# All splits of the streamed weights on VectorE, instead of one in eight (one in six) on GpSimd

## The chip, the cores and the metric

The kernel runs on one core of a Trainium2 chip. The metric is the device time in microseconds (us) of one execution. The engines that matter are TensorE (PE in the views; its weight loads are PEld), VectorE (DVE), ScalarE (ACT), GpSimd (POOL) and SyncE (SP), whose queue issues nearly all transfers. SBUF is the on-chip memory, PSUM the accumulators that TensorE writes.

## The reference

One sequence of 256 rows of width 1024, in float32, goes through two blocks. The first has two layers: retention, then differential attention, each with attention to a memory of 256 rows beside it and a feed-forward part behind it. The second has a mixer of a gated delta rule and a gated linear attention, a cross-attention, and an MLP. Cut to what matters:

```python
for layer in range(2):
    u = rms_norm(x, attn_norm_w[layer]) @ w_in[layer]
    o_main = retention(...) or diff_attention(...)          # chunks of 64 rows
    o_mem = memory_attention(qc, mk, mv)
    x = x + concatenate([o_main, o_mem]) @ w_out[layer]
    gu = rms_norm(x, ffn_norm_w[layer]) @ w_gate_up[layer]
    x = x + (silu(gu[..., :2816]) * gu[..., 2816:]) @ w_down[layer]
# second block
proj = rmsnorm(x, norm_mix_g) @ w_in
qkv = silu(causal_depthwise_conv(concatenate([gq, gk_, gv]), gdn_conv_w))   # four taps
o_a = gated_delta_rule_chunked(q_a, k_a, v_a, g_a, beta_a)
o_b = gla_chunked(q_b, k_b, v_b, log_fg)
merged = sigmoid(gate_a) * y_a + sigmoid(gate_b) * y_b
x = x + merged @ w_out
x = x + cross_attention(x, mem) @ xattn_wo
x = x + square(relu(rmsnorm(x) @ mlp_w1)) @ mlp_w2
return rmsnorm(x, norm_final_g)
```

All products are wanted at float32 accuracy.

## The kernel before

**Weights.** Some 213 MB of weights come from HBM, each used once, in units of 128 x 2 x 512 numbers (two rows of blocks of 128, 512 columns). The function `unit` (L261) makes one: SyncE issues the transfer into a buffer `raw` (three of them), ScalarE casts it to the matmul's shorter float format as `hi` (L277; four buffers), and then `lo = raw - hi`, the remainder in the same format (four buffers), is made through the helper `tt` (L184, its instruction is L185). This last step is called the split here. TensorE then makes three products of each block with an activation that is split in the same way: hi with xh, lo with xh, hi with xl (`mm`, L207). `proj` (L290), `proj_T` and `proj_T2` loop over the units of one weight matrix, so TensorE goes through 12 or more matmuls for each unit.

**Who splits.** A counter `lo_count` chooses the engine of each split: GpSimd for every eighth unit (`share`), for every sixth from the mixer's convolution on (L782) until the mixer's end (L825); VectorE for the others. GpSimd's other work is the inverse roots (`rsqrt`, L200: a power on a few numbers for each row, named `tiny`), some masks (L1005) and fills, and two products of 128x1024.

**Order.** Each engine has a queue of its own and runs it in order. The program is written stage by stage, and a scheduler puts the instructions of each engine into an order before the kernel is built, from the data dependencies, the buffers and its own estimate of durations. So a change of one instruction's engine moves others.

**Held evacuations.** Three places (L432, L461, L677) call `later(instruction, n)`: the product that scales attention heads by their inverse root (T_699 is one, in `mem_kv`) is kept back on VectorE until the split of the n-th next unit, four for the first half of the rows and five for the second. They are released in `unit`, but in the kernel before only if that unit's split is itself on VectorE; if it is GpSimd's turn, they wait for the next unit.

**Names.** T, L, Z, B, G, H, V are work tiles in SBUF, `acc` and `ps` accumulators in PSUM, `constants` a tile with the identity and other fixed numbers. A `ps<-constants,...` matmul is a transpose (L210).

Of the kernel before, what the change touches and what calls it, by code (L numbers as in the profile page):

```python
# [34 lines left out]
class _Pack:  # L35
    def __init__(self):
        self.parts, self.at = [], 0
# [83 lines left out]
class _Builder:  # L121
    def __init__(self, ctx, tc, aps, names, stages):
        self.tc = tc
        self.nc = tc.nc
        self.a = dict(zip(names, aps))
        self.stages = stages
        self.n = self.np = 0
        ent = lambda name, bufs, **k: ctx.enter_context(tc.tile_pool(name=name, bufs=bufs, **k))
        self.cp = ent("const", 1)
        self.sp = ent("stream", 4)  # L130
        self.wp = ent("work", 1)
        self.tp = ent("tiny", 1)
        self.dp = ent("scratch", 2, space=bass.MemoryType.DRAM)
        self.pa = ent("acc", 4, space=PSUM)
        self.ps = ent("small", 2, space=PSUM)
        self.lo_count = 0
        self.mT2 = self.xv = self.xT = None
        self.share = 8
        self.n2 = 0
        self.units, self.held = 0, {}  # L140
        self.use('T', ('sm', 'pg'))
# [119 lines left out]
    def unit(self, w, k0, nk, cols):  # L261
        nc = self.nc
        W = sum(b for _, b in cols)
        self.n += 1
        n = self.n
        raw = self.sp.tile([P, 2, 512], F32, tag="raw", name=f"raw{n}", bufs=3)
        parts = [slice(0, 1), slice(1, 2)] if self.units == 0 else [slice(0, nk)]
        for k in parts:
            o = 0
            for c0, wd in cols:  # L270
                nc.sync.dma_start(out=raw[:, k, o:o + wd], in_=w[(k0 + k.start) * P:(k0 + k.stop) * P, c0:c0 + wd]
                                  .rearrange("(k p) c -> p k c", p=P))
                o += wd
        hi = self.sp.tile([P, 2, 512], F32R, tag="hi", name=f"hi{n}", bufs=4)
        lo = self.sp.tile([P, 2, 512], F32R, tag="lo", name=f"lo{n}", bufs=4)
        for k in parts:
            nc.scalar.copy(hi[:, k, :W], raw[:, k, :W])  # L277
        self.lo_count += 1
        eng = nc.gpsimd if self.lo_count % self.share == 0 else nc.vector
        for k in parts:  # L280
            last = self.tt(lo[:, k, :W], raw[:, k, :W], hi[:, k, :W].bitcast(F32), ALU.subtract, eng=eng)
        self.units += 1
        if eng is nc.vector:
            for u in [u for u in self.held if u <= self.units]:
                for i in self.held.pop(u):
                    self.tc.add_manual_dep(i, last.ins.name, mybir.DependencyInfo(
                        mybir.DependencyClass.NoSync, mybir.DependencyReason.DATA), reason="queued behind a split")
        return hi, lo

    def proj(self, hT, w, cols, order=None, meanwhile=None):  # L290
# [476 lines left out]
    def mixer(self):  # L767
        nc, w = self.nc, self.a['w_in_2'][0]
        ms, r = self.stats(self.x)
        xn = [self.big() for _ in range(2)]  # L770
        for t in range(2):
            for c in range(2):
                cc = slice(c * 512, (c + 1) * 512)
                self.ts(xn[t][:, cc], self.x[t][:, cc], r[:, t:t + 1])
        hT = self.x_T2('mix', 0, xn)
        hT[7]
        if self.mT2 is not None:
            self.xv = self.xattn_v(self.mT2)
        self.gates(hT)
        decays = [self.decays(g) for g in range(2)]  # L780
        self.use('G', ('sm',))
        self.share = 6  # L782
        z = [[self.conv(hT, w, kind, g) for kind in range(3)] for g in range(2)]
        on = []
        self.use('T', ('pg',))
        for g in range(2):
            on.append(self.gdn(g, z[g], *decays[g]))
        self.use('G', ('sm',))
        obn = self.gla(hT, w)
        oaT = []  # L790
        for g in range(2):
            a = self.proj(hT, w, [(3072 + g * 512, 512)])
            e = [self.t('L') for _ in range(2)]
            for t in range(2):
                self.act(e[t], a[t], AF.Tanh, scale=0.5)
                self.stt(e[t], e[t], 1.0, a[t], ALU.add, ALU.mult)
                self.tt(e[t], e[t], on[g][t])
            oaT += self.to_T(lambda t, f: e[t][:, f * P:(f + 1) * P], 4, 'Z', lambda f: self.col('gdn'))
        for c in range(2):
            a = self.proj(hT, w, [(6160 + c * 512, 512)])  # L800
            for t in range(2):
                e = self.t()
                self.act(e, a[t], AF.Tanh, scale=0.5)
                self.stt(e, e, 1.0, a[t], ALU.add, ALU.mult)
                self.tt(obn[t][c], obn[t][c], e)
        m = [[self.t('L') for _ in range(2)] for _ in range(2)]
        ga = [[self.t('L') for _ in range(2)] for _ in range(2)]
        for c0, d in ((8224, m), (7200, ga)):
            for c in range(2):
                g = self.proj(hT, w, [(c0 + c * 512, 512)])  # L810
                for t in range(2):
                    self.act(d[t][c], g[t], AF.Tanh, scale=0.5)
        for c in range(2):
            y = self.proj(oaT, self.a['w_branch_gdn_2'][0], [(c * 512, 512)])
            for t in range(2):
                self.stt(ga[t][c], ga[t][c], 1.0, y[t], ALU.add, ALU.mult)
        obT = self.to_T(lambda t, f: obn[t][f // 4][:, (f % 4) * P:(f % 4 + 1) * P], 8, 'H',
                        lambda f: self.col('gla', f % 2))
        for c in range(2):
            y = self.proj(obT, self.a['w_branch_gla_2'][0], [(c * 512, 512)])  # L820
            for t in range(2):
                self.stt(m[t][c], m[t][c], 1.0, y[t], ALU.add, ALU.mult)
                self.tt(m[t][c], m[t][c], ga[t][c], ALU.add)
        self.use('T', ('sm', 'pg'))
        self.share = 8  # L825
        mT = self.to_T(lambda t, f: m[t][f // 4][:, (f % 4) * P:(f % 4 + 1) * P], 8, 'Z')
        self.xT = self.out_proj(mT, self.a['w_out_2'][0], 0.5, gname='xat')

# [593 lines left out]
```

## Time and profile before

| | before |
|---|---|
| median of three timed runs | 1295.37 us (1294.4 to 1302.5) |
| the profiled execution's own time | 1287.81 us |
| its span | 1286.1 us |
| TensorE busy | 1250.5 us (97%) |
| TensorE weight loads | 1071.6 us (83%) |
| VectorE busy | 828.1 us (64%), 1299 instructions |
| ScalarE busy | 678.8 us (53%) |
| GpSimd busy | 180.9 us (14%), 115 instructions |

The profile is of one execution. A busy share is an average over stages with different limits: what a change is worth shows in the stretches in which TensorE stands still, and in what it waits for there.

### The profile page before, as it was taken

Reading aid. Unit: us, or ns where it says so; the run is one execution under the profiler, and the core shown is the slowest. Engines: PE = TensorE matmul, PEld = TensorE weight load, DVE = VectorE, ACT = ScalarE, POOL = GpSimd, SP = SyncE. Lnnn points to the kernel's source line nnn. Section 1 sums busy time; section 2 is a strip of 40 time slices with the busy share of each in tenths; the row PEclk is TensorE's granted clock in tenths of the full one; section 3 lists DMA queues with packets and bytes.
Section 4 is the critical chain, followed back from the end, with each engine's and each line's share of the span. In section 5 each row is a group of like instructions: output and inputs, shape, how many; then the busy total and the mean of one; then the engine's idle time right before and its main releaser. Section 6 shows DMA issues by size and latency. Waiting matters only on the chain.

```text
span 1286.1 us, 19034 instructions
## 1 busy us (share of the span) xinstructions
PE 1250.5 (97%) x7160; PEld 1071.6 (83%) x7160; DVE 828.1 (64%) x1299; ACT 678.8 (53%) x1088; POOL 180.9 (14%) x115
## 2 busy tenths in 40 slices
PE   8999999999999999999998999999999999999997
PEld 8787888888778888888878998867788897888886
DVE  6576677755876667674467787486635665788542
ACT  5655656545664565554467573343344444565442
POOL 0122110010420110100101021221111000001011
PEclk9999999999999999999999999999999999999999
DMA  8826566656644256665653545224365552565653
GB/s 297 279 87 203 176 196 185 196 195 192 187 131 148 83 164 201 192 190 189 195 176 115 181 121 170 84 70 142 112 194 175 172 177 86 166 207 178 201 190 107
DMA packets 147005, 215.72 MB, mean 168 GB/s; under 512 B 15456, under 2 KB 71904, under 8 KB 146912
## 3 DMA queue, kind: packets, MB, share of 16 engines
q1 hardware_dynamic: 146336, 213.27, 53.3%
q8 instruction: 56, 0.92, 0.3%
q10 hardware_dynamic: 432, 0.70, 0.2%
q0 software_dynamic: 144, 0.52, 0.1%
q14 instruction: 37, 0.30, 0.1%
HBM read 213.02 MB, written 1.44 MB: 167 GB/s over the span
## 4 chain that ended last, share of the span: by engine, by line
PE 84%; DVE 6%; DMA 3%; ACT 3%; issue 2%; POOL 1%; SPq 1%; POOLq 0%; ACTq 0%; DVEq 0%
PE acc L207 74%; PE ps L207 7%; PE ps L210 2%; DVE lo L185 2%; ACT hi L277 1%; DVE T L185 1%; DMA raw<-in_w_in_dram 1%; POOL tiny L200 1%; DVE L L185 1%; ACT T L195 1%; SPq L1053 0%; DMA constants<-in_small_dram 0%; DVE B L185 0%; DMA B<-in_mem_dram 0%; SPq L1029 0%
## 5 line engine op out<-in xcount | busy, mean ns | idle before, releaser
L277 ACT CAST hi<-raw 128x1024 fp32r<-128x1024 f32 (+1 forms) x393 | 407.1, 1039 | 413.3 <-PE acc L207 326.7
L185 DVE TENSOR_TENSOR lo<-raw,hi 128x1024 fp32r<-128x1024 f32 (+1 forms) x341 | 412.5, 1214 | 316.5 <-ACT hi L277 312.3
L207 PE MATMUL acc<-H,hi 128*128 128x512 f32 (+1 forms) x1696 | 470.5, 347 | 1.8 <-ACT hi L277 1.7
L207 PE MATMUL acc<-H,lo 128*128 128x256 f32 x1328 | 372.2, 281 | 0.0
L207 PEld LDWEIGHTS acc<-H,hi 128*128 128x128 f32 x1696 | 296.3, 190 | 43.7 <-ACT hi L277 2.5
L207 PEld LDWEIGHTS acc<-H,lo 128*128 128x128 f32 x1328 | 252.4, 190 | 1.8 <-issue 0.8
L185 POOL TENSOR_TENSOR lo<-raw,hi 128x1024 fp32r<-128x1024 f32 (+1 forms) x52 | 124.2, 2389 | 796.2 <-ACT hi L277 618.8
L207 PE MATMUL acc<-hi,H 128*128 128x512 f32 (+1 forms) x672 | 212.4, 392 | 1.2 <-ACT H L195 0.6
L207 PE MATMUL acc<-hi,Z 128*128 128x512 f32 x544 | 171.4, 391 | 0.0
L207 PE MATMUL acc<-hi,L 128*128 128x512 f32 x512 | 160.2, 390 | 0.0
L207 PEld LDWEIGHTS acc<-hi,H 128*128 128x128 f32 x672 | 125.3, 189 | 27.9 <-issue 1.8
L207 PE MATMUL acc<-lo,H 128*128 128x512 f32 (+1 forms) x336 | 131.6, 392 | 0.8 <-DVE lo L185 0.8
L207 PEld LDWEIGHTS acc<-hi,Z 128*128 128x128 f32 x544 | 102.1, 188 | 20.9
L207 PEld LDWEIGHTS acc<-hi,L 128*128 128x128 f32 x512 | 96.1, 188 | 19.8
L207 PE MATMUL acc<-lo,Z 128*128 128x512 f32 x272 | 106.0, 390 | 0.0
L207 PE MATMUL acc<-lo,L 128*128 128x512 f32 x256 | 99.7, 390 | 0.0
L207 PEld LDWEIGHTS acc<-lo,H 128*128 128x128 f32 x336 | 63.6, 189 | 14.6 <-DVE lo L185 1.7
L200 POOL TENSOR_TENSOR tiny<-tiny,constants 128x2 f32<-128x2 f32 (+4 forms) x41 | 41.4, 1012 | 238.6 <-DVE tiny L189 190.2
L207 PEld LDWEIGHTS acc<-lo,Z 128*128 128x128 f32 x272 | 51.1, 188 | 10.2
L207 PEld LDWEIGHTS acc<-lo,L 128*128 128x128 f32 x256 | 48.1, 188 | 9.8
L357 ACT COPY T<-acc 128x256 f32<-128x256 f32 x120 | 43.8, 369 | 12.8 <-PE acc L207 9.3
L185 DVE TENSOR_TENSOR T<-acc,T 128x256 f32<-128x256 f32 x120 | 44.9, 416 | 2.1 <-ACT T L357 2.1
(218 smaller groups left out, 1109.3 us busy)
## 6 DMA issues: line engine op xcount, KB each, us to landing
raw<-in_w_in_dram SPq DMA_DIRECT2D x91, 512.0 KB, 3.7
raw<-in_w_gate_up_dram SPq DMA_DIRECT2D x176, 256.0 KB, 3.4
raw<-in_mlp_w_dram SPq DMA_DIRECT2D x64, 512.0 KB, 4.3
raw<-in_w_down_dram SPq DMA_DIRECT2D x44, 512.0 KB, 4.5
raw<-in_w_out_dram SPq DMA_DIRECT2D x24, 512.0 KB, 4.3
raw<-in_w_in_dram SPq DMA_DIRECT2D x42, 256.0 KB, 3.9
raw<-in_w_mem_kv_dram SPq DMA_DIRECT2D x8, 512.0 KB, 3.9
raw<-in_xattn_wk_dram SPq DMA_DIRECT2D x8, 512.0 KB, 3.8
```

The lines of the kernel that those rows point to most:

```text
L185: return (eng or self.nc.vector).tensor_tensor(out=out, in0=a, in1=b, op=op)
L195: self.nc.scalar.activation(out, in_, f, scale=scale, bias=bias, **k)
L200: self.nc.gpsimd.tensor_tensor(out=out, in0=in_, in1=self.c('mhalf')[:, :n], op=ALU.pow)
L207: self.nc.tensor.matmul(out, lhsT, rhs, start=start, stop=stop, skip_group_check=True)
L210: self.nc.tensor.transpose(out, in_, self.ident[:in_.shape[0], :in_.shape[0]])
L277: nc.scalar.copy(hi[:, k, :W], raw[:, k, :W])
L357: self.nc.scalar.copy(out[:, a, :], accs[a][:, 1, :])
```

## The change

Every split is VectorE's. The counter and the two shares go, and with them the condition on the release of held evacuations, which now always come with the unit they were meant for. What is computed is the same.

```diff
@@ __init__
-        self.lo_count = 0
         self.mT2 = self.xv = self.xT = None
-        self.share = 8
@@ unit
         for k in parts:
             nc.scalar.copy(hi[:, k, :W], raw[:, k, :W])
-        self.lo_count += 1
-        eng = nc.gpsimd if self.lo_count % self.share == 0 else nc.vector
+        eng = nc.vector
         for k in parts:
             last = self.tt(lo[:, k, :W], raw[:, k, :W], hi[:, k, :W].bitcast(F32), ALU.subtract, eng=eng)
         self.units += 1
-        if eng is nc.vector:
-            for u in [u for u in self.held if u <= self.units]:
-                for i in self.held.pop(u):
-                    self.tc.add_manual_dep(...)
+        for u in [u for u in self.held if u <= self.units]:
+            for i in self.held.pop(u):
+                self.tc.add_manual_dep(...)
@@ mixer
-        self.share = 6
@@
-        self.share = 8
```

Fifty-two instructions move from GpSimd's queue to VectorE's, 51 of 128x1024 and one of 128x2x256. The numbers of instructions on TensorE, ScalarE and SyncE stay. Lines in the changed kernel are two lower up to L275 and four to six lower behind it. The scheduler's order changes in more places than the 52. Three of them follow.

First, VectorE's queue in the differential attention, at the softmax's scale factors (tiny_3387 scales T_3369, which TensorE then transposes into ps_3391). Before:

```order
L185 TENSOR_TENSOR Z_3347<-acc_3254,tiny_3345 128x512
L708 RECIPROCAL tiny_3387<-tiny_3372 128x2
L192 SCALAR_TENSOR_TENSOR tiny_3233<-tiny_3371 128x2
L451 TENSOR_REDUCE tiny_3410<-T_3404 128x2
L192 SCALAR_TENSOR_TENSOR tiny_3387<-tiny_3387,tiny_3230,tiny_3371 128x2
L189 TENSOR_SCALAR tiny_3410<-tiny_3410 128x2
L192 SCALAR_TENSOR_TENSOR T_3369<-T_3370,tiny_3387,T_3369 128x128 x2
```

After:

```order
L183 TENSOR_TENSOR Z_3347<-acc_3254,tiny_3345 128x512
L704 RECIPROCAL tiny_3387<-tiny_3372 128x2
L190 SCALAR_TENSOR_TENSOR tiny_3233<-tiny_3371 128x2
L447 TENSOR_REDUCE tiny_3410<-T_3404 128x2
L190 SCALAR_TENSOR_TENSOR tiny_3387<-tiny_3387,tiny_3230,tiny_3371 128x2
L187 TENSOR_SCALAR tiny_3410<-tiny_3410 128x2
L183 TENSOR_TENSOR lo_3640<-raw_3637,hi_3639 128x1024
L190 SCALAR_TENSOR_TENSOR T_3369<-T_3370,tiny_3387,T_3369 128x128 x2
```

The split lo_3640 was GpSimd's and now stands ahead of T_3369. On TensorE, the transpose ps_3391 stood ahead of the last two matmuls of unit 3478 (hi_3478, lo_3479), and now stands behind the first three of the next unit, 3497.

Second, TensorE's queue early in the first layer, where the memory's keys (T_699) are transposed into ps_719 between the products of units 899, 917 and 935. Before:

```order
L207 MATMUL acc_896<-lo_900,H_104 128x512
L207 MATMUL acc_896<-hi_899,H_104 128x512
L207 MATMUL acc_895<-hi_917,H_144 128x512
L207 MATMUL acc_895<-lo_918,H_144 128x512
L207 MATMUL acc_895<-hi_917,H_144 128x512 x2
L207 MATMUL acc_895<-lo_918,H_144 128x512
L207 MATMUL acc_895<-hi_917,H_144 128x512
L207 MATMUL acc_896<-hi_917,H_144 128x512
L207 MATMUL acc_896<-lo_918,H_144 128x512
L207 MATMUL acc_896<-hi_917,H_144 128x512
L210 MATMUL ps_719<-constants,T_699 128x128
```

After:

```order
L205 MATMUL acc_896<-lo_900,H_104 128x512
L205 MATMUL acc_896<-hi_899,H_104 128x512
L208 MATMUL ps_719<-constants,T_699 128x128
L205 MATMUL acc_895<-hi_917,H_144 128x512
L205 MATMUL acc_895<-lo_918,H_144 128x512
L205 MATMUL acc_895<-hi_917,H_144 128x512 x2
L205 MATMUL acc_895<-lo_918,H_144 128x512
L205 MATMUL acc_895<-hi_917,H_144 128x512
L205 MATMUL acc_896<-hi_917,H_144 128x512
L205 MATMUL acc_896<-lo_918,H_144 128x512
L208 MATMUL ps_719<-constants,T_699 128x128 x3
```

The first transpose moved up by nine matmuls, to the start of unit 917. On VectorE, the first half of T_699 stood behind the split lo_980 and now stands directly behind lo_954, which was GpSimd's.

Third, VectorE's queue at the end of the gated linear attention, where T_8127, T_8146 and a root (tiny) lead to L_8901 and L_8902, which TensorE transposes into ps_8909. Before:

```order
L189 TENSOR_SCALAR tiny_8124<-tiny_8124 128x4
L185 TENSOR_TENSOR T_8127<-ps_8114,tiny_8124 128x512
L185 TENSOR_TENSOR L_8901<-L_8901,T_8127 128x512
L1128 TENSOR_REDUCE tiny_8140<-T_8138 128x4
L192 SCALAR_TENSOR_TENSOR G_9087<-G_9087,acc_9013 128x512
L192 SCALAR_TENSOR_TENSOR tiny_8140<-tiny_8140,tiny_7833 128x4
L185 TENSOR_TENSOR L_8663<-L_8663,G_9087 128x512
L189 TENSOR_SCALAR tiny_8143<-tiny_8143 128x4
L192 SCALAR_TENSOR_TENSOR G_9091<-G_9091,acc_9014 128x512
L185 TENSOR_TENSOR T_8146<-ps_8129,tiny_8143 128x512
L185 TENSOR_TENSOR L_8721<-L_8721,G_9091 128x512
L185 TENSOR_TENSOR L_8902<-L_8902,T_8146 128x512
```

After:

```order
L183 TENSOR_TENSOR lo_9202<-raw_9199,hi_9201 128x1024
L183 TENSOR_TENSOR T_8112<-ps_8103,tiny_7835 128x512
L1122 TENSOR_REDUCE tiny_8121<-T_8119 128x4
L190 SCALAR_TENSOR_TENSOR tiny_8121<-tiny_8121,tiny_7833 128x4
L187 TENSOR_SCALAR tiny_8124<-tiny_8124 128x4
L183 TENSOR_TENSOR T_8127<-ps_8114,tiny_8124 128x512
L183 TENSOR_TENSOR L_8901<-L_8901,T_8127 128x512
L1122 TENSOR_REDUCE tiny_8140<-T_8138 128x4
L190 SCALAR_TENSOR_TENSOR tiny_8140<-tiny_8140,tiny_7833 128x4
L187 TENSOR_SCALAR tiny_8143<-tiny_8143 128x4
L183 TENSOR_TENSOR T_8146<-ps_8129,tiny_8143 128x512
L183 TENSOR_TENSOR L_8902<-L_8902,T_8146 128x512
```

The four operations on G_9087, G_9091, L_8663 and L_8721 stand earlier now, outside this chain; the split lo_9202, of a unit that TensorE needs four units later, stands ahead of T_8112, where before lo_9144 stood.

Elsewhere, in words: the split lo_6755 of the mixer's gates now stands behind all products T_6533 to T_6565 of the decays; lo_4382 stands in front of the reciprocal of tiny_4018; and at the start of the gated delta rule TensorE's small products (ps_7433 to ps_7485) moved up by as much as nine units, in between the products of the convolution.

## Rows read from the trace of the kernel before

**Rows 1.** The page: busy time by engine, its share of the span, instructions.

```profile
PE 1250.5 (97%) x7160; PEld 1071.6 (83%) x7160; DVE 828.1 (64%) x1299; ACT 678.8 (53%) x1088; POOL 180.9 (14%) x115
```

**Rows 2.** Grouped waits of TensorE: line waited for: us in total, times, longest.

```profile
PE acc L207 <- DVE lo L185: 0.8, 2, 0.5
```

**Rows 3.** Stretches: busy us by engine, granted clock (PEclk), DMA share, GB/s.

```profile
150.00:200.00 50.00, 50.00 (x291) 44.05 (x290) 37.93 (x47) 30.33 (x47) 5.73 (x3) 1.00 0.63 191
...
680.00:690.00 10.00, 6.63 (x36) 5.85 (x35) 9.31 (x13) 5.76 (x10) 2.51 (x1) 0.83 0.20 65
...
1200.00:1250.00 50.00, 50.00 (x222) 41.42 (x221) 21.39 (x22) 20.80 (x23) 7.18 (x3) 1.00 0.61 190
```

The columns between the commas are PE, PEld, DVE, ACT and POOL.

**Rows 4.** Groups by form, GpSimd: xcount, busy us, mean ns, idle before.

```profile
L185 POOL TENSOR_TENSOR lo<-raw,hi 128x1024 fp32r<-128x1024 f32 x51 | 122.9, 2411 | 794.8 <-ACT hi L277 617.4 <-DVE T L185 97.0 <-DVE T L192 57.5
```

**Rows 5.** Groups by form, VectorE.

```profile
L185 DVE TENSOR_TENSOR lo<-raw,hi 128x1024 fp32r<-128x1024 f32 x332 | 406.5, 1228 | 312.7 <-ACT hi L277 308.6 <-PE acc L207 3.6
...
L185 DVE TENSOR_TENSOR T<-T,T 128x512 f32<-128x512 f32 x22 | 21.8, 989 | 3.8 <-ACT T L195 1.8
...
L185 DVE TENSOR_TENSOR T<-T,row 128x512 f32<-128x512 f32 x22 | 15.0, 680 | 0.0
...
L189 DVE TENSOR_SCALAR tiny<-tiny 128x2 f32<-128x2 f32 x42 | 7.4, 178 | 4.6 <-POOL tiny L200 4.0
```

**Rows 6.** Timelines at 350 us: start, duration, engine, what, in brackets the idle time before.

```profile
350.22 2.37 POOL L185 TENSOR_TENSOR lo<-raw,hi 128x1024 fp32r<-128x1024 f32 x1 [3.18 <-ACT hi L277]
...
350.86 1.74 DVE L192 SCALAR_TENSOR_TENSOR tiny<-tiny,tiny,tiny 128x2 f32<-128x2 f32 x1
...
353.04 0.59 PE L210 MATMUL ps<-constants,T 128*128 128x128 f32 x2 [1.86 <-DVE T L192]
```

**Rows 7.** Timelines at 411 us.

```profile
411.60 1.23 DVE L192 SCALAR_TENSOR_TENSOR tiny<-tiny,tiny,tiny 128x2 f32<-128x2 f32 x1
...
413.40 0.44 PE L210 MATMUL ps<-constants,T 128*128 128x128 f32 x2 [0.62 <-DVE T L192]
```

**Rows 8.** Timelines at 682 us.

```profile
681.90 2.90 DVE L189 TENSOR_SCALAR L<-L 128x512 f32<-128x512 f32 x2
...
685.53 0.50 PE L207 MATMUL ps<-T,T 128*128 128x512 f32 x1 [3.37 <-DVE T L185]
```

**Rows 9.** Timelines at 862 us.

```profile
862.66 1.97 DVE L185 TENSOR_TENSOR T<-T,T 64x60 f32<-64x60 f32 x1
...
865.28 0.88 PE L210 MATMUL ps<-constants,L 128*128 128x128 f32 x6 [1.56 <-DVE L L185]
```

**Rows 10.** Timelines at 881 us.

```profile
881.47 3.21 DVE L185 TENSOR_TENSOR B<-T,constants 128x1024 f32<-128x1024 f32 x1 [1.79 <-DMA T<-dr]
...
884.74 1.44 PE L207 MATMUL ps<-B,B 128*128 128x64 f32 x11 [1.52 <-DVE B L185]
```

**Rows 11.** Timelines at 921 us.

```profile
921.03 1.94 DVE L185 TENSOR_TENSOR L<-L,G 128x512 f32<-128x512 f32 x1
...
923.63 0.87 PE L210 MATMUL ps<-constants,L 128*128 128x128 f32 x6 [1.82 <-DVE L L185]
```

**Rows 12.** Timelines at 1052 us, in the cross-attention.

```profile
1051.97 2.40 POOL L185 TENSOR_TENSOR lo<-raw,hi 128x1024 fp32r<-128x1024 f32 x1 [11.63 <-ACT hi L277]
...
1052.83 2.62 DVE L185 TENSOR_TENSOR lo<-raw,hi 128x1024 fp32r<-128x1024 f32 x1 [1.27 <-ACT hi L277]
...
1068.31 0.33 PE L210 MATMUL ps<-constants,T 128*128 128x128 f32 x1 [0.87 <-ACT T L195]
```

**Rows 13.** Timelines at 67 us: a cast, the roots, the first ps_719.

```profile
65.67 1.05 ACT L277 CAST hi<-raw 128x1024 fp32r<-128x1024 f32 x1 [0.83 <-DMA raw<-in_w_in_dram]
...
66.21 1.98 POOL L200 TENSOR_TENSOR tiny<-tiny,constants 128x4 f32<-128x4 f32 x2 [8.48 <-DVE tiny L189]
...
69.04 0.27 PE L210 MATMUL ps<-constants,T 128*128 128x128 f32 x1
```

**Rows 14.** Timeline of VectorE at 749 us.

```profile
749.45 4.76 DVE L192 SCALAR_TENSOR_TENSOR Z<-acc,constants,Z 128x255 f32<-128x255 f32 x12
```

More of the change, by code (lines that the diff above doesn't have):

```diff
@@ L282, in unit @@
         self.units += 1
-        if eng is nc.vector:
-            for u in [u for u in self.held if u <= self.units]:
-                for i in self.held.pop(u):
-                    self.tc.add_manual_dep(i, last.ins.name, mybir.DependencyInfo(
-                        mybir.DependencyClass.NoSync, mybir.DependencyReason.DATA), reason="queued behind a split")
+        for u in [u for u in self.held if u <= self.units]:
+            for i in self.held.pop(u):
+                self.tc.add_manual_dep(i, last.ins.name, mybir.DependencyInfo(
+                    mybir.DependencyClass.NoSync, mybir.DependencyReason.DATA), reason="queued behind a split")
         return hi, lo
```

## The prediction

> **What bounds the kernel now.** The page's busy times come first [rows 1]: TensorE is busy 1250.5 of 1286.1 us, VectorE 828.1, GpSimd 180.9. So a microsecond of VectorE or GpSimd counts only where TensorE stands still for it. Next the grouped waits of TensorE [rows 2]: in the whole span it waited 0.8 us for a split made by VectorE, and no line of that view names GpSimd at all. The splits themselves, on either engine, are ahead of TensorE. Then the table of stretches [rows 3]: in 150 to 200 us (the first feed-forward part) TensorE is busy 50.00 of 50.00 with VectorE at 37.93, while in 680 to 690 it is busy 6.63 of 10.00 with VectorE at 9.31. The time to be won or lost lies in such short stretches between the long matrix products, where a chain of small VectorE operations feeds TensorE.
>
> The timelines of these stretches show why VectorE is late there. At 350.22 GpSimd begins a split of 2.37 us, which ends at 352.59. VectorE begins an operation on 128x2 numbers at 350.86 and needs 1.74 us, to 352.60: it ends with GpSimd's split [rows 6]. The 42 operations of the nearest small form have a mean of 178 ns [rows 5]. TensorE then waits 1.86 us for what VectorE made next. The same picture, a small operation of unusual length, stands at 681.90, 862.66, 881.47, 921.03 and 1052.83 [rows 8 to 12]. So a VectorE operation that reads its inputs from SBUF and starts while GpSimd splits does not run until that split ends. The Trainium skill, page "SBUF — State Buffer", section "SBUF: two separate sides", says the same of a port pair that the two engines share as an exclusive lock, held for the whole instruction; these rows agree.
>
> **The change part by part.**
>
> *What VectorE takes over.* 52 splits leave GpSimd: 51 of 128x1024 and one of half that size. On GpSimd one took 2411 ns [rows 4], on VectorE 1228 [rows 5]. Added work: 51 x 1.228 + 0.6 = 63.2 us.
>
> *What VectorE gets back.* The blocked operations disappear. The group means show some of it: T<-T,T on 128x512 costs 989 ns against 680 for T<-T,row of the same size [rows 5], 22 x 0.309 = 6.8 us, and the six blocked operations of rows 6 and 8 to 12 show an excess of 1.6, 1.5, 1.8, 2.0, 1.3 and 1.4 us (worked out below), 9.6 us; together some 16 us. The lower bound for the whole is this 16 us; the upper, if each of the 52 splits blocks one operation for half its length, is 52 x 1.2 = 62 us. VectorE thus ends at 828 + 63 - 16 = 875 us at most, 68% of the span, and at least at 829. I take 865.
>
> *What that costs in the long stretches.* Nothing: there VectorE has 12 of 50 us free [rows 3], two or three splits more are 2.5 to 3.7 us, and TensorE's queue has work of up to four units ahead. If that cover went, each split would cost up to its 1.2 us; TensorE's 0.8 us of waits for splits [rows 2] speaks against it.
>
> *What is won in the short stretches*, one by one, each bounded by TensorE's own wait:
> - 353.04 us [rows 6]: wait 1.86. VectorE gains 1.6 and has split lo_3640 (1.2) put in front of T_3369, a net of 0.4; but TensorE's new order puts five more matmuls of 0.23 us (222 fill 50 us [rows 3]) in front of ps_3391, 1.15. Together 1.6; bounds 0.4 and 1.9.
> - 413.40 [rows 7]: wait 0.62 behind an operation of 1.23 us; the split goes into a stretch where VectorE idled. 0.6; bounds 0 and 0.6.
> - 685.53 [rows 8]: wait 3.37. The two TENSOR_SCALARs took 2.90; at 0.68 each, the nearest row of this size [rows 5], 1.36. In the new order the split (lo_6755) stands behind the whole chain. 1.5; bounds 1.5 and 3.4.
> - 865.28 [rows 9]: wait 1.56, operation 1.97 instead of about 0.2. 1.6; bounds 0.4 (if its split of 1.2 stands ahead) and 1.6.
> - 884.74 [rows 10]: wait 1.52, operation 3.21 instead of 1.23 (the split, of the same size). 1.5.
> - 923.63 [rows 11]: wait 1.82, operation 1.94 instead of 0.68; the new order also takes the G operations out of the chain to L_8902. 1.8; bounds 1.3 and 1.8.
> - 1068.31 [rows 12]: wait 0.87, and two smaller ones behind it. VectorE's split at 1052.83 took 2.62 instead of 1.23, and the raw buffer behind GpSimd's split comes free 1.2 us earlier. 1.0; bounds 0 and 1.4.
> Sum 9.6 us, bounds 5 and 12.
>
> *What is lost.* The splits now stand in VectorE's queue, which runs in order, and the new order differs from the old in more places than the 52.
> - About 67 us [rows 13]: T_699 is scaled by a root that GpSimd makes until 68.19; TensorE used it at 69.04 without a wait. The evacuation is now released one unit earlier, TensorE has the transpose ps_719 right behind unit 900 (nine matmuls of 0.23 us earlier, at about 66.9 by the old clock), and VectorE has lo_954 ahead of T_699. The split's cast ends at 66.72, the split at about 68.0, T_699 at 68.4. New wait 68.4 - 66.9 = 1.5; bounds 0 and 2.
> - About 750 [rows 14]: VectorE makes twelve tap sums in a row, 4.76 us without a gap. The new order moves the small products of the delta rule up between the convolution's units, where their inputs queue behind those sums. I take 2.0; bounds 0 and 4.8, the twelve sums' length.
> - About 916: lo_9202 stands ahead of T_8112. Its buffer comes free with the last matmul on hi_9125, which is in the middle of ps_8103; the cast 1.05 (as at 65.67 [rows 13]), the split 1.2 and T_8112 0.7 make 3.0 us against some 1.7 us of TensorE work up to the product that needs T_8112. New wait 1.3; bounds 0 and 2.2.
> Sum 4.8, bounds 0 and 9.
>
> Net 9.6 - 4.8 = 4.8 us less. The profiled execution took 1287.81 us, 7.6 under the median of the timed runs, 1295.37. The sum gives 1283.0 for the former; by the same difference the median goes to 1290.6. I predict 1290.
>
> **The rivals.**
>
> *Nothing to be seen.* The losses cancel the gains, or TensorE's waits move to what is late next (at 685.53 the wait of 3.37 is only partly the lock's). For it: the first wait of a chain hides the second, and a different order makes new ones. Against: seven waits have an operation behind them that ends with GpSimd's split. Time 1295, from 1293 to 1298.
>
> *Slower: a split that isn't ready holds up VectorE's queue.* GpSimd waited 617.4 us for casts before its splits [rows 4], which cost nobody anything; the same wait in VectorE's queue holds up whatever stands behind. Outside the stretches in which TensorE is fed all the time there are 14 of the 52 splits (68, 328 to 410, 658, 682, 766 to 920, 1052 us). If each puts its 1.23 us into the chain that TensorE waits for, 17.2 us are lost and 9.6 won: 1295.4 + 7.6 = 1303. It decides from 8 of the 14 on (8 x 1.23 = 9.8 > 9.6). For it: the three places above are of this kind, and VectorE is at 9.31 of 10.00 at 680 to 690. Against: at 410 and 682 the new order has the split in an idle time or behind the chain. The Trainium skill, page "Perfetto Trace Analysis", section "Optimizing Scalar/DVE Operations", advises handing work of a saturated VectorE to other engines, GpSimd too, which speaks for the old kernel in such stretches; it adds that it may not help between these two, as they share a port. No run here yet shows which of the two holds.
>
> *More is won.* All waits of rows 6 to 12 go in full (11.6 us by their rows), and TensorE's granted clock, at 0.83 in 680 to 690 [rows 3], stays at 1.00 there, which is up to 1.7 us more; the losses don't come. 1295.4 - 13.3 = 1282.
>
> *The change isn't what it says*: the order of the instructions shows no split left on GpSimd and the same number of transfers, so this is out.
>
> **How the numbers follow.** My forecast, -8 to -2 us: 0.45. Nothing, within 2.5 of 1295: 0.2. Slower, 1298 to 1310: 0.22. More, 1279 to 1287: 0.13. The forecast's own range is 1287 to 1293. The range of 8 in 10 reaches from 1280 to 1302: it leaves out 0.06 below and the upper half of the slower case, 0.11. A change of under 1% (13 us) can't well be told from none with this kernel, whose three runs lie from 1294.4 to 1302.5. Faster by over that (under 1282.4) is most of the last case, 0.10; slower by over that (above 1308.3) only if more than the whole sum of the slower case comes together, 0.06; the rest, 0.84, lies within.
>
> **What would show it right or wrong.** In the profile after: GpSimd's busy time down to about 57 us (180.9 less 122.9 and 1.3), VectorE's at 845 to 875; no operation of 0.2 or 0.7 us that takes 1.7 or more, and the group T<-T,T at 0.68 us. TensorE's waits at the seven places gone or down by the amounts above; a new wait for T at the first ps_719, one in the delta rule's start, and one at the product behind T_8112. The long stretches still at 50.00 of 50.00. Wrong would be: lines of TensorE waiting for a split of VectorE of more than some 3 us in all (the slower case), waits of the same length at the seven places under another name (then the lock was not what set them), or a stretch of the feed-forward parts under 49.9.

## The result

The changed kernel takes 1281.0 us (median of four runs, 1280.7 to 1282.9), the kernel before 1296.5 (four runs, 1294.4 to 1302.5): a ratio of 0.9887 with a 95% interval of 0.9861 to 0.9913. In a second set, six runs of it against 23 of the kernel before, it was 1282.2 against 1294.4, ratio 0.9904 (0.9881 to 0.9928). So it is faster by 1.0 to 1.1%, 12 to 15.5 us. The forecast was 1290, faster by some 5: the sign was right, and the range of 8 in 10 (1280 to 1302) held by one microsecond; the forecast's own range, 1287 to 1293, did not hold, and the size was under half. The time is that of the rival "more is won", which had a chance of 0.13.

The profiled execution took 1280.81 us, with a span of 1279.1. The busy times of its page, which answer to [rows 1]:

```profile
PE 1248.9 (98%) x7160; PEld 1069.3 (84%) x7160; DVE 852.6 (67%) x1351; ACT 679.8 (53%) x1088; POOL 55.2 (4%) x63
```

GpSimd is down to 55.2 us (forecast 57) and VectorE up by 24.5 to 852.6 (forecast 845 to 875, taken as 865). The groups by form of VectorE, beside [rows 5]:

```profile
L183 DVE TENSOR_TENSOR lo<-raw,hi 128x1024 fp32r<-128x1024 f32 x383 | 467.4, 1224 | 299.8 <-ACT hi L275 295.6 <-PE acc L205 2.8
...
L183 DVE TENSOR_TENSOR T<-T,T 128x512 f32<-128x512 f32 x22 | 15.2, 693 | 3.3 <-ACT T L193 1.0 <-DVE T L183 0.5
...
L183 DVE TENSOR_TENSOR T<-T,row 128x512 f32<-128x512 f32 x22 | 15.0, 681 | 0.0
```

T<-T,T fell from 989 to 693 ns, next to its twin of the same size: no operation of this group is blocked any more. TensorE's grouped waits, the largest before:

```profile
PE ps L210 <- DVE L L185: 4.9, 4, 1.8
PE ps L210 <- DVE T L185: 3.6, 5, 1.8
...
PE ps L207 <- DVE T L185: 3.4, 1, 3.4
...
PE ps L210 <- DVE T L192: 2.5, 2, 1.9
```

and after, with the one for splits that answers to [rows 2]:

```profile
PE ps L208 <- DVE T L183: 5.2, 9, 1.4
PE ps L208 <- ACT T L193: 3.3, 3, 1.4
...
PE ps L208 <- DVE L L183: 2.5, 3, 1.0
...
PE acc L205 <- DVE lo L183: 0.8, 2, 0.5
```

All lines of that view add up to 27.8 us before and 22.5 after. VectorE's splits, 52 more of them, are waited for as little as before: 0.8 us. For GpSimd's roots, which stood in one queue with the splits, VectorE waited no less than before; the line before and after:

```profile
DVE tiny L189 <- POOL tiny L200: 13.5, 17, 1.2
```

```profile
DVE tiny L187 <- POOL tiny L198: 14.0, 17, 1.2
```

The stretches, beside [rows 3]:

```profile
150.00:200.00 50.00, 50.00 (x291) 44.09 (x290) 38.10 (x51) 30.88 (x46) 0.00 (x0) 1.00 0.66 199
...
680.00:690.00 10.00, 8.79 (x62) 7.97 (x62) 9.83 (x21) 9.28 (x17) 0.00 (x0) 1.00 0.19 54
...
1200.00:1250.00 50.00, 50.00 (x222) 41.42 (x221) 24.85 (x25) 20.54 (x23) 0.00 (x0) 1.00 0.64 194
```

In the long stretches TensorE is as full as before; at 680 to 690 its busy time rose from 6.63 to 8.79 of 10 and the granted clock from 0.83 to 1.00, with VectorE at 9.83.

Between these two executions the span fell by 7.0 us: 5.3 are waits (27.8 - 22.5), and 1.6 are TensorE's own busy time (1250.5 - 1248.9). The other 5 to 8.5 us of the measured difference are not in this pair of profiles at all. Where they are was the question of the experiments.

### The profile page after: what moved, and what is told of

It reads as the page before. It is cut to its first block, busy times and chain, and to the rows that moved or that the text cites. A ratio compares the mean times of both kernels' runs of the same rounds, so it can differ in the third digit from the quotient of the medians.

```text
span 1279.1 us, 19025 instructions
## 1 busy us (share of the span) xinstructions
PE 1248.9 (98%) x7160; PEld 1069.3 (84%) x7160; DVE 852.6 (67%) x1351; ACT 679.8 (53%) x1088; POOL 55.2 (4%) x63
## 4 chain that ended last, share of the span: by engine, by line
PE 82%; DVE 6%; DMA 5%; ACT 2%; issue 2%; POOL 2%; SPq 1%; POOLq 0%; ACTq 0%; DVEq 0%
PE acc L205 73%; PE ps L205 6%; PE ps L208 2%; DVE lo L183 2%; POOL tiny L198 1%; ACT hi L275 1%; DMA raw<-in_w_in_dram 1%; DMA raw<-in_w_mem_kv_dram 1%; DVE T L183 1%; DMA V<-in_mem_2T_dram 1%; DVE L L183 1%; DMA T<-dr 0%; ACT T L193 0%; SPq L1047 0%; DMA raw<-in_w_out_dram 0%
## 5 line engine op out<-in xcount | busy, mean ns | idle before, releaser
L183 DVE TENSOR_TENSOR lo<-raw,hi 128x1024 fp32r<-128x1024 f32 (+1 forms) x393 | 474.0, 1210 | 303.1 <-ACT hi L275 298.7
L275 ACT CAST hi<-raw 128x1024 fp32r<-128x1024 f32 (+1 forms) x393 | 407.6, 1038 | 430.7 <-PE acc L205 313.4
L183 DVE TENSOR_TENSOR T<-T,T 128x512 f32<-128x512 f32 (+10 forms) x88 | 29.2, 334 | 4.2 <-ACT T L193 1.0
```

What stands on the lines that cost most here:

```text
L183: return (eng or self.nc.vector).tensor_tensor(out=out, in0=a, in1=b, op=op)
```

## The experiments

Two theories stood against each other. A: GpSimd's splits block VectorE, this counts only in the short stretches, and it is a fixed loss. B: the loss varies from one execution to the next. Two rivals stood against both: that the gain came from the new order, or that VectorE's added work costs something that a better gain hides.

### The kernel before once more

> The kernel before, unchanged, once more: how far its timed runs spread, and whether its profiled execution again lies some 8 us under its timed median (1287.8 against 1296.5), which the changed kernel's does not (1280.8 against 1281.0). Theory A (the time is lost in some short stretches where VectorE is blocked by GpSimd's split, the same in each execution): all runs within 3 us of each other, ratio 1.000. Theory B (GpSimd's splits have a length or a place that varies from execution to execution, so that the loss varies): runs spread over 5 us or more, 1288 to 1302, and the profile's stalls differ from those of the first profile.

Measured: 1295.4 us, 12 runs from 1287.3 to 1300.2, ratio 0.9994 (0.9968 to 1.0021). The spread is that of B: the same program varies by 13 us, the changed one by 2 to 4.5. Over these 12 executions the span goes, with some scatter, with TensorE's mean granted clock: a span of 1285.6 us at 0.998, 1291.6 at 0.994, 1294.0 at 0.991, 1298.5 at 0.984, some 920 us for a whole unit of clock between the two ends (12.9 / 0.014). The mean clock was 0.992 over the 35 executions of the kernel before that were timed beside one another, and 0.996 over the six of the changed kernel; by that line the difference of 0.004 is worth about 4 us, an estimate. The first profile, with 1287.81 us and a clock of 0.996, was one of the best executions of the kernel before: of 69 others in the experiments one was quicker.

The second profile took 1293.31 us, nearer to the median, with a span of 1291.6:

```profile
PE 1253.7 (97%) x7160; PEld 1073.8 (83%) x7160; DVE 830.6 (64%) x1299; ACT 679.0 (53%) x1088; POOL 181.9 (14%) x115
```

Against the changed kernel's profile this span is 12.5 us longer, which is the size of the measured gain: 7.6 us in TensorE's waits (30.1 against 22.5, all lines of the view) and 4.8 in TensorE's own busy time (1253.7 against 1248.9). Most of the waits are as in the first profile, as A had it: those of 1.86, 3.37, 1.56, 1.52 and 1.82 us [rows 6 and 8 to 11] are 1.93, 3.36, 1.54, 1.51 and 1.83 here. What differs most between the two executions is one wait, shown below, and the clock.

Where the clock fell differs from execution to execution. Stretches of the second profile:

```profile
355.00:360.00 5.00, 4.40 (x18) 3.29 (x19) 3.18 (x8) 3.00 (x7) 0.14 (x1) 1.00 0.42 126
685.00:690.00 5.00, 3.48 (x11) 3.00 (x12) 5.00 (x10) 2.40 (x6) 0.17 (x1) 0.66 0.38 105
800.00:805.00 5.00, 3.98 (x21) 3.60 (x22) 0.96 (x1) 0.00 (x0) 1.43 (x1) 0.77 0.45 98
...
885.00:890.00 5.00, 3.49 (x20) 3.00 (x19) 1.85 (x1) 0.00 (x0) 3.22 (x3) 0.80 0.65 188
```

Here 355 to 360 ran at 1.00, and 800 and 885 did not. In the first profile of the same kernel it was the other way round:

```profile
355.00:360.00 5.00, 5.00 (x19) 3.95 (x18) 3.39 (x7) 2.83 (x7) 0.28 (x1) 0.66 0.33 88
...
800.00:805.00 5.00, 5.00 (x31) 4.39 (x30) 0.00 (x0) 0.22 (x1) 2.77 (x2) 1.00 0.67 201
...
885.00:890.00 5.00, 5.00 (x31) 4.43 (x31) 1.58 (x3) 1.48 (x3) 2.83 (x2) 1.00 0.86 309
```

A mean of 0.66 is part of the stretch at 2.4 GHz and part at 1.2. The timeline of TensorE in the first profile shows the lower level behind the wait of 1.86 us at 353.04 [rows 6], and then the higher one again:

```profile
356.12 1.05 PE L207 MATMUL acc<-hi,H 128*128 128x512 f32 x2
...
358.61 0.63 PE L207 MATMUL acc<-hi,H 128*128 128x512 f32 x2
```

Two matmuls of the same form take 1.05 us and then 0.63. Which waits such a stretch follows differs: in the first profile those of 1.86 and 3.37 us at 353 and 685, and not that of 1.52 at 884; in the second those of 3.36, 1.08 and 1.51 us at 686, 801 and 886. The second profile kept its clock behind a wait of 1.93 us at the place of [rows 6]:

```profile
355.60 0.59 PE L210 MATMUL ps<-constants,T 128*128 128x128 f32 x2 [1.93 <-DVE T L192]
```

Nor does each such stretch have a wait ahead of it: in the profile of a variant of the changed kernel that comes last below (the product on VectorE), the mean clock was 0.66 from 670 to 675 us, and the nearest wait ahead of it that the timeline lists was one of 0.61 us at 644.8:

```profile
670.00:675.00 5.00, 5.00 (x26) 4.40 (x25) 4.13 (x12) 1.60 (x3) 0.00 (x0) 0.66 0.12 46
```

The block itself varies, too. Second profile, VectorE and TensorE at 68 us, beside [rows 13]:

```profile
68.44 2.66 DVE L185 TENSOR_TENSOR lo<-raw,hi 128x512 fp32r<-128x512 f32 x1 [1.71 <-ACT hi L277]
...
71.48 0.33 PE L210 MATMUL ps<-constants,T 128*128 128x128 f32 x1 [1.70 <-DVE T L185]
```

In the first profile this small split began before GpSimd's and took 0.69 us; here it came 0.6 us later, fell behind GpSimd's and took 2.66, and TensorE waited 1.70 us for ps_719 where it had not waited at all.

### One half of the splits at a time

```diff
-        eng = nc.gpsimd if self.lo_count % self.share == 0 else nc.vector
+        eng = nc.gpsimd if self.lo_count % self.share == 0 and self.long else nc.vector
```

with `self.long` true in the two feed-forward parts and the MLP; the other kernel has `not self.long`.

> The 25 splits of the feed-forward parts and the MLP stay on GpSimd, the other 27 are VectorE's. Theory A: TensorE is fed all the time in these parts, a blocked VectorE operation costs nothing there; the time is that of the changed kernel, ratio 0.987 to 0.991 (1280 to 1285 us). Rival (a split on GpSimd costs wherever it stands, or the gain is spread over the whole span): about half of the gain, ratio 0.993 to 0.996.

> The 27 splits outside the feed-forward parts and the MLP stay on GpSimd, the 25 inside are VectorE's. Theory A: the blocked operations that delay TensorE are all still there; the time is that of the kernel before, ratio 0.998 to 1.002 (1293 to 1299 us). Rival (the gain is spread over the whole span): about half of the gain, ratio 0.993 to 0.996.

> The changed kernel, unchanged, beside the two halves on the same chip: ratio 0.986 to 0.991, runs within 3 us of each other.

Measured: 1283.6 us for GpSimd in the long stretches only, ratio 0.9916 (0.9894 to 0.9938); 1296.0 for GpSimd in the others only, 1.0006 (0.9988 to 1.0024); 1282.2 for the changed kernel beside them. The busy times, first of the long ones, then of the others:

```profile
PE 1252.3 (98%) x7160; PEld 1070.8 (83%) x7160; DVE 839.6 (65%) x1326; ACT 678.8 (53%) x1088; POOL 114.9 (9%) x88
```

```profile
PE 1252.6 (97%) x7160; PEld 1072.4 (83%) x7160; DVE 843.8 (65%) x1324; ACT 680.2 (53%) x1088; POOL 120.8 (9%) x90
```

VectorE without any block would have 852.6 less its share of the splits: 852.6 - 25 x 1.22 = 822 and 852.6 - 27 x 1.22 = 820. So it lost 18 us to blocks in the long stretches and 24 in the others. The 18 cost 1.4 us of time (1283.6 - 1282.2), which can't be told from nothing, as the runs of either kernel spread over 4 to 5 us; the 24 cost 13.8, as much as all 52 splits within the noise (1294.4 - 1282.2 = 12.2). In the long stretches TensorE has matmuls at hand while VectorE is blocked, in the others it waits.

### Twice the splits on GpSimd

```diff
-        self.share = 8        # and 6 in the mixer
+        self.share = 4        # and 3 in the mixer
```

> The kernel before with twice as many splits on GpSimd (every fourth unit, every third in the mixer: 105 instead of 52). Theory A (VectorE operations blocked behind GpSimd's splits in the short stretches, and TensorE's clock that falls after the waits): more blocked operations, time 1300 to 1315 us, mean granted clock under that of the kernel before (0.992), VectorE's busy time about 800 us. Rival (relieving VectorE is worth something, the changed kernel won by another order of its queue): 1285 to 1295 us.

Measured: 1307.0 us, ratio 1.0081 (1.0053 to 1.0108), mean granted clock 0.990 in the profile, and VectorE as expected:

```profile
PE 1258.5 (97%) x7160; PEld 1076.0 (83%) x7160; DVE 798.2 (61%) x1246; ACT 677.4 (52%) x1088; POOL 311.0 (24%) x168
```

Reckoned as above, VectorE lost 73 us to blocks (852.6 - 105 x 1.21 = 725), against 39 in the kernel before (852.6 - 63.2 = 789 against 828.1). In time: 1281 to 1282 without, 1294 to 1297.5 with 52 splits, 1307 with 105. The second dose cost 9.4 us (1307.0 against 1297.5 of the kernel before, timed beside it), somewhat less than the 12 to 15.5 of the first.

### Neither GpSimd nor VectorE

```diff
-            last = self.tt(lo[:, k, :W], raw[:, k, :W], hi[:, k, :W].bitcast(F32), ALU.subtract, eng=eng)
+            if (self.lo_count + 1) % self.share == 0:
+                last = nc.scalar.copy(lo[:, k, :W], raw[:, k, :W])
+            else:
+                last = self.tt(lo[:, k, :W], raw[:, k, :W], hi[:, k, :W].bitcast(F32), ALU.subtract, eng=eng)
```

> The changed kernel, but the splits of the same 52 units are replaced by a plain cast on ScalarE (the subtraction is left out there, lo is a second copy of the weights): neither GpSimd's lock nor the 52 more splits on VectorE. If those splits cost nothing on VectorE (my step on the long stretches): the time of the changed kernel, 1279 to 1285 us. If VectorE's added 63 us cost something: faster than the changed kernel, 1272 to 1278. ScalarE gets 52 x 1.05 = 55 us more, which could itself cost a few us in the stretches where it feeds TensorE (432 us).

Measured: 1281.3 us, ratio 0.9875 (0.9837 to 0.9913): the changed kernel's time.

```profile
PE 1249.4 (98%) x7160; PEld 1070.8 (84%) x7160; DVE 794.2 (62%) x1299; ACT 727.2 (57%) x1140; POOL 56.3 (4%) x63
```

VectorE has 58 us less to do than in the changed kernel, and it brings nothing that can be measured. ScalarE has 47 us more, which could hide a gain; but TensorE's waits for ScalarE did not grow (6.4 us against 6.9), and those for VectorE stayed (15.3 against 15.6). So the 52 splits cost nothing on VectorE that these runs can see, as the step on the long stretches had it, and in the short ones too.

### The block alone, with the order unchanged

```diff
+        if self.lo_count % self.share == 0:
+            spare = ...                       # one tile of 128x2x512
+            for k in parts:
+                self.tt(spare[:, k, :W], raw[:, k, :W], hi[:, k, :W].bitcast(F32), ALU.subtract, eng=nc.gpsimd)
```

and, in the second kernel, `nc.gpsimd.memset(spare[:, :, :W], 0.0)` three times in its place. The first keeps the order of the four other engines throughout; with the fills some neighbours change places before 116 us.

> The changed kernel with the order of TensorE's, VectorE's, ScalarE's and SyncE's instructions unchanged, and GpSimd makes the splits of the old 52 units once more, into a spare tile that nobody reads (two of the fourteen T buffers are given up for it, which by itself changes no order). VectorE's work is that of the changed kernel. Theory A (it is the blocking alone): the time goes back to that of the kernel before or over it, 1290 to 1305 us, VectorE's busy time goes from 852.6 up by 25 to 40 us, its small operations take 1.2 to 2.2 us behind the splits again, and the clock falls to about 0.992. Rival (the gain came from the new order of the queues and the earlier release): 1279 to 1284 us.

> The same, but in the place of each redundant split GpSimd fills the spare tile three times with zeros (some 2.9 us, longer than a split), which writes SBUF and reads nothing. If what blocks VectorE is GpSimd's reading from SBUF: the time of the changed kernel, 1279 to 1284 us, and no long operations on VectorE. If any long GpSimd instruction blocks it: as with the redundant splits, 1290 to 1310.

Measured for the redundant splits: 1321.4 us, ratio 1.0217 (1.0181 to 1.0254), 39 us more than the changed kernel and above the 1290 to 1305 of the expectation; VectorE's busy time rose by 59 us, not 25 to 40. Busy time, two groups of VectorE by form, and the timelines of GpSimd, VectorE and TensorE at the place of [rows 6]:

```profile
PE 1265.6 (96%) x7160; PEld 1078.5 (82%) x7160; DVE 911.3 (69%) x1351; ACT 678.9 (52%) x1088; POOL 217.3 (16%) x115
...
L184 DVE TENSOR_TENSOR lo<-raw,hi 128x1024 fp32r<-128x1024 f32 x383 | 488.9, 1280 | 270.2 <-ACT hi L276 268.9
...
L184 DVE TENSOR_TENSOR T<-T,T 128x512 f32<-128x512 f32 x22 | 20.3, 921 | 2.8 <-ACT T L194 0.5 <-DVE T L184 0.5
...
362.59 2.39 POOL L184 TENSOR_TENSOR spare<-raw,hi 128x1024 fp32r<-128x1024 f32 x1 [3.18 <-ACT hi L276]
...
363.24 1.76 DVE L191 SCALAR_TENSOR_TENSOR tiny<-tiny,tiny,tiny 128x2 f32<-128x2 f32 x1
...
366.52 0.59 PE L209 MATMUL ps<-constants,T 128*128 128x128 f32 x2 [1.88 <-DVE T L191]
```

With every queue but GpSimd's in the changed kernel's order, the blocked operation (1.76 us, to the end of the split at 364.98) and TensorE's wait (1.88) are back as they were. So the new order alone does not give the gain. What it is worth by itself no run measured, but three kernels with other orders, the changed one, the one with GpSimd in the long stretches only and the one with the casts, lie within 3 us, and the one with GpSimd in the others only gained nothing. Why the redundant splits cost more than the 12 to 15.5 us of the kernel before was not tested. GpSimd's copy needs the same cast as VectorE's own split, and VectorE's splits took 489 us instead of 467, 22 of the 59 us that it lost (911.3 - 852.6); the raw buffer is also held until both are done.

Measured for the fills: 1292.8 us, ratio 0.9979 (0.9959 to 0.9998). The time is in the range of the second reading, but there is no block as by the redundant splits. VectorE's groups by form, a line of TensorE's grouped waits, the stretches, and the timelines of GpSimd and VectorE at one place:

```profile
L184 DVE TENSOR_TENSOR lo<-raw,hi 128x1024 fp32r<-128x1024 f32 x383 | 467.3, 1224 | 302.7 <-ACT hi L276 301.6
...
L184 DVE TENSOR_TENSOR T<-T,T 128x512 f32<-128x512 f32 x22 | 15.2, 692 | 3.0 <-ACT T L194 1.0
...
L188 DVE TENSOR_SCALAR tiny<-tiny 128x2 f32<-128x2 f32 x42 | 10.7, 256 | 4.0 <-POOL tiny L199 3.4
...
PE acc L206 <- DVE lo L184: 6.3, 5, 3.0
...
0.00:100.00 100.00, 89.79 (x506) 76.54 (x507) 61.61 (x112) 53.55 (x100) 84.77 (x96) 0.98 0.62 203
100.00:200.00 100.00, 93.82 (x500) 79.93 (x501) 71.36 (x104) 55.33 (x86) 73.87 (x78) 0.98 0.59 180
200.00:300.00 100.00, 100.00 (x538) 86.57 (x537) 67.04 (x87) 54.20 (x78) 0.00 (x0) 1.00 0.62 193
...
79.34 2.97 POOL L284 MEMSET spare<- 128x1024 f32 x3
...
80.55 0.78 DVE L188 TENSOR_SCALAR tiny<-tiny 128x2 f32<-128x2 f32 x1
```

A fill waits for no other engine, so the 156 ran in the first 180 us, with GpSimd 85 of the first 100 us busy. VectorE's two-input TENSOR_TENSORs kept their 1224 and 692 ns; of the 383 splits, 48 lie in the first 186 us, with a mean of 1223. Its small TENSOR_SCALARs, one input each, did not: the group of 42 has a mean of 256 ns against 178 [rows 5], the one at 80.55 ends at 81.33, with the second of the three fills from 79.34 on, and VectorE's busy time is 857.7 against 852.6. The time is lost in that part: a matmul that starts at 186.3 us in the changed kernel starts at 198.6 here, 12.3 later, and from there to the end (1260.5 and 1275.0) only 2.2 come to it. Two things are late there, and no run tells them apart: the roots, which stand behind fills in GpSimd's queue (one that starts at 66.02 us in the changed kernel starts at 70.36 here), and these small operations. So an instruction of GpSimd that only writes does not block a TENSOR_TENSOR with two inputs from SBUF, though it held up small TENSOR_SCALARs; one that reads two inputs blocked both. The Trainium skill, page "SBUF — State Buffer", section "SBUF: two separate sides", limits the lock against two-input operations of VectorE to operations of GpSimd that read SBUF; the two runs agree with that.

### Two small edits on the changed kernel

```diff
-        for c, (ct, full, eng) in enumerate(((cT, T, nc.vector), (cU, U, nc.gpsimd))):
+        for c, (ct, full, eng) in enumerate(((cT, T, nc.vector), (cU, U, nc.vector))):
@@ the other: mem_kv, mem_q, diff_layer
-  self.later(..., (4, 5)[t])
+  self.later(..., (5, 6)[t])
```

> The changed kernel, and also the one product of 128x1024 that GpSimd makes in each half of the gated delta rule (the second of the two with the block mask, 1.93 us at 799.65) goes to VectorE (1.23 us). Theory A: where GpSimd's result itself is waited for (TensorE at 803, 0.65 us) the wait goes down by up to 0.7 us in each of the two halves: 1279 to 1282 us, at the edge of what can be measured. Rival (VectorE's queue is the limit there): no change or 1 to 2 us slower.

> The changed kernel, with the held evacuations released one unit later (5 and 6 instead of 4 and 5 units on). The changed kernel's new wait at the first ps_719 (0.55 us in its first profile, 1.02 in its second) should go, and the waits at 98.5, 101.7 and 114.4 us (1.58, 0.48, 0.67) go down if they have the same cause: 1.0 to 3 us less, 1278 to 1281 us. If they go and the time stays, the waits only moved to the next transpose.

> Both small edits together on the changed kernel: the gated delta rule's second masked product on VectorE, and the held evacuations released one unit later. If the two gains of about 1 us each add up: 1278 to 1280 us; rival (they are noise): 1280 to 1283.

Measured: 1280.2 (0.9867, 0.9832 to 0.9901), 1280.1 (0.9869, 0.9837 to 0.9901) and, both together, 1281.0 us (0.9893, 0.9865 to 0.9921). None can be told from the changed kernel. With the product on VectorE the waits at 797 and 803 us went from 1.18 and 0.49 to 0.33 and none, and one at 860 from 0.28 to 1.20. With the later release the wait at the first ps_719 is gone, and one at 117.6 us is 1.34 us long, where the changed kernel's timeline has 0.33 and 0.52 at 101.7 and 114.4: it moved to the next transpose. So the unit at which a held evacuation is released, which the change also touched, makes no difference here that can be seen.

## Why the prediction was right, and where it was too small

**The mechanism was right.** VectorE is held up behind GpSimd's splits; this counts only where a chain of small operations feeds TensorE; the splits cost nothing measurable on VectorE (the cast on ScalarE in their place brought nothing); and the order alone was not the cause (the redundant splits bring the waits back in the same order). One reading was too strict: at these places only the operations on 128x2 and 64x60 numbers end with GpSimd's split. The larger ones end 0.3 to 1.1 us behind it, as at 1052.83 [rows 12], where the split ends at 1054.37 and the operation at 1055.45; they run behind it. And VectorE got back 39 us (63.2 - 24.5), where 26 were taken, within the bounds of 16 and 62.

**The waits, place by place.** The changed kernel's timelines of VectorE and TensorE, beside [rows 6], [rows 8] and [rows 11]:

```profile
353.31 0.21 DVE L190 SCALAR_TENSOR_TENSOR tiny<-tiny,tiny,tiny 128x2 f32<-128x2 f32 x1
...
355.06 0.59 PE L208 MATMUL ps<-constants,T 128*128 128x128 f32 x2 [0.33 <-DVE T L190]
...
680.45 0.76 DVE L187 TENSOR_SCALAR L<-L 128x512 f32<-128x512 f32 x2
...
681.93 0.50 PE L205 MATMUL ps<-T,T 128*128 128x512 f32 x1 [1.22 <-DVE T L183]
...
921.27 0.87 PE L208 MATMUL ps<-constants,L 128*128 128x128 f32 x6 [0.87 <-DVE L L183]
```

| place before [rows] | wait before | after | won | forecast |
|---|---|---|---|---|
| 353 [6] | 1.86 | 0.33 | 1.5 | 1.6 |
| 413 [7] | 0.62 | none | 0.6 | 0.6 |
| 685 [8] | 3.37 | 1.22 | 2.2 | 1.5 |
| 865 [9] | 1.56 | none | 1.6 | 1.6 |
| 884 [10] | 1.52 | none | 1.5 | 1.5 |
| 923 [11] | 1.82 | 0.87 | 1.0 | 1.8 |
| 1068 [12] | 0.87 | 0.67 | 0.2 | 1.0 |
| sum | 11.6 | 3.1 | 8.5 | 9.6 |

At 685 the two TENSOR_SCALARs take 0.76 us together, not 1.36: the nearest row of that size, a two-input product, was too dear for a one-input operation. At 921 the chain is late next: a root of GpSimd's (to 919.48), three operations of VectorE behind it, to 921.2. In the cross-attention the wait is for ScalarE and hardly moved.

**The losses** were put at 4.8. At the first ps_719 the chain came out as worked out, but TensorE came later than by the old clock:

```profile
67.68 0.42 DVE L183 TENSOR_TENSOR T<-acc,tiny 128x256 f32<-128x256 f32 x1
...
68.15 0.33 PE L208 MATMUL ps<-constants,T 128*128 128x128 f32 x1 [0.39 <-DVE T L183]
```

0.39 us instead of 1.5; and the kernel before pays 1.70 there in its second profile. At 750 to 770 there is no wait, and none at the product behind T_8112 (2.0 and 1.3 forecast). Not foreseen were 0.33 and 0.52 us at 101.7 and 114.4, 0.32 and 0.52 at 829 and 832, half a microsecond more at 345 (0.91, 0.45 before), and as much in the delta rule's first half, where the waits for B are 1.7 us in all (1.2 before). The two sums agree, 4.8 us net forecast and 5.3 measured in the waits of the two profiles, but partly by luck: the gains came to 1.1 us less than forecast and the losses to 1.6 less (8.5 - 5.3 = 3.2), and two of the three places named for a loss had none.

**The step that failed** is the last one: "by the same difference the median goes to 1290.6". It carried the 7.6 us between the profiled execution and the median over as if they were a constant of the kernel. They were part of the effect: the changed kernel's profile (1280.8) and median (1281.0) coincide. The profile that I had was one of the best executions of the kernel before, and I took the table of stretches, where the clock was 0.83 at 680 to 690, for a rival of 1.7 us alone. The runs put two things in that place. The clock is lower on average than in that profile, 0.992 against 0.996, about 4 us by the line through the twelve runs; in the second profile TensorE's busy time is 3.2 us longer than in the first (1253.7 against 1250.5). And whether a VectorE operation falls behind a split can hang on 0.6 us, so that another execution has waits that this profile had not: 2.3 us more in the second (30.1 against 27.8), 1.70 of it at ps_719. The spread of the three runs shown, 8 us, was read as noise of the measurement only; it was a sign of a loss that varies. That the waits bring the lower clock is read from the timelines, from the common run of clock and span, and from the changed kernel's higher clock; no experiment held the clock and kept the waits, and one stretch of lower clock shown above has no such wait ahead of it. So this part of the cause is argued, not shown.

**The rivals.** The slower one, splits that hold up VectorE's queue, is answered by the cast on ScalarE: taking them off again wins nothing, and TensorE waits for VectorE's splits no longer than before (0.8 us). "Nothing to be seen" is out by both intervals. "More is won" has the time, but its conditions hold only in part: the clock at 680 to 690 is 1.00, as it said, but 8.5 of the 11.6 us of waits went, and 3.2 us of new ones came.

## What to carry to other kernels

A few operations handed to GpSimd can cost VectorE more than half of the time that they save it: here 63 us of splits taken off cost 39 us of blocks, and some of the blocks fell on the chains that TensorE waits for. Where VectorE has room in the long stretches, keep GpSimd's long two-input work out of the short ones, or off GpSimd altogether. Before carrying a difference of one profile over to a median, ask why the two differ: a spread between runs and a mean clock under 1.00 can be the cost of the very thing that is changed.

## What the runs showed of the hardware that I had not expected

The same program's span varied by 13 us over twelve executions, for the most part in step with the mean granted clock of TensorE (0.984 to 0.998). Of two equal waits of 1.9 us one was followed by a stretch at half speed, the other was not. And 156 fills on GpSimd, 0.95 us each and back to back for much of 180 us, left VectorE's two-input TENSOR_TENSORs at 1224 and 692 ns but lengthened its small TENSOR_SCALARs (256 ns against 178 in the group of 42; 5 us over all of VectorE's operations), while 52 splits there lengthened the operations of VectorE by 39 us in all.
